# Weight splits, block-diagonal weights, rotation, modulation and skip products taken off GpSimd in a two-layer hybrid backbone

## The chip, the cores and the metric

The kernel runs on one core of one Trainium2 chip. The metric is the device time of one execution in microseconds. Before the change it is 1362.43 us, the median of three runs (1362.07 to 1367.08). The core has TensorE (matmuls into PSUM), VectorE (DVE), ScalarE (ACT), GpSimd (POOL) and SyncE (SP, which here only issues DMAs). Each has its own instruction stream, and they wait for each other by semaphores.

## The reference, cut to what matters

A diffusion backbone of two layers over 256 latent tokens behind 256 context tokens, of width 1024, all in float32:

```python
for layer in range(DEPTH):                    # DEPTH = 2
    mod = split(silu(c) @ ada_w[layer] + ada_b[layer], 6)   # for c and for c_ctx
    h = rmsnorm(x, norm_mix_w[layer]) * (1 + mod[1]) + mod[0]
    if layer % 2 == 0:   # 16 SSD heads in 4 groups beside 4 retention heads
        y = ssd_retention_mixer(h, ...)       # q, k rotated: x1 * cos - x2 * sin, ...
        #   y_ssd = scan + d_skip[:, None] * xs
    else:                # mLSTM: conv, block-wise q, k, v (512 blocks of 4 x 4), gated scan
        y = mlstm_mixer(h, ...)
    x = x + mod[2] * y
    hf = rmsnorm(x, norm_ffn_w[layer]) * (1 + mod[4]) + mod[3]
    x = x + mod[5] * ((silu(hf @ w1) * (hf @ w3)) @ w2)     # hidden width 2816
return rmsnorm(latent part of x, final_norm_w)
```

## The kernel before, in words

All 512 tokens stay in SBUF, features on the 128 partitions (`xt`, eight tiles of 128 x 512). A float32 product is made of three passes: every weight tile and every activation is split into a rounded high part and the rest (`H` and `L`), and `mm3` adds H·H, H·L and L·H in PSUM (lines 407 to 409; `mm` in the profile).

Weights come as 248 tiles of 128 x 1024 in the order of the list `plan`. `wload` issues a tile's DMA on SyncE's queue into one of three buffers `wraw`; `wprep` lets ScalarE write the high part `wH` (line 367) and VectorE or GpSimd the rest `wL` (line 368, through the helper `tt`, line 227). `wnext` keeps up to three split tiles ahead. Which engine makes `wL` is set by the tile's number:

```python
on_pool = {nz + i for i in (-15, -13, -11, -8, -6, -3, 9, 19, 25)} | {12, 14, 15, 31, 43, 56, 70, 71, 74}
...
tt(G if wpos[0] - len(wraws) - 1 in on_pool else V, L, raw, f32v(H), ALU.subtract)
```

So 18 tiles go to GpSimd. `G`, `V`, `S` and `TE` are GpSimd, VectorE, ScalarE and TensorE.

The start works through the eight feature chunks of the first normalized input in the order 3, 0, 4, 1, 5, 2, 6, 7. A chunk needs its shift and scale for both streams, four products of a weight tile with the conditioning vector. For chunks 0 to 2 TensorE makes them (`ada_rows`, line 302). For chunks 3 to 7 `ada_split` makes them, each either as one VectorE instruction that also sums over the columns (`junk<-adaf,cbc`, line 291, followed by a read of the sum) or as a GpSimd product into `ada` that ScalarE sums (line 296). The tuple `units` says how many of the four are VectorE's. Then VectorE scales the chunk (`xn`, line 487), ScalarE writes its high part (`hH`, line 497) and VectorE the rest (`hL`, line 498), and TensorE multiplies four weight tiles by it. The later modulation vectors are VectorE's in any case (`junk<-ada,cbc`, line 267).

Layer 0 then runs a list of units: projections of an SSD group or a retention head, or a quarter of the output projection. Between their matmuls `slot` advances generators that hold the scans. In `ssd_scan`, `xtok` is the group's x by tokens, `vw` its weighted copies for the states, `comb` the decay matrices times the scores, `y` (`yssd` in the profile) starts as the skip product `d_skip * x`. GpSimd also masks the decay rows (`erow`, line 750). In `ret_qk`, q and k of a head (`qkraw`) are multiplied by the cosines, a copy with swapped halves (`qksw`) by the sines.

Layer 1 has 16 feature tiles. `ml_post` runs the depthwise convolution (`conv<-xp`, line 685: four VectorE instructions per tile), splits the result (`xcH`, `xcL`) and calls `build_bd`, which spreads a tile's 4 x 4 blocks into a block-diagonal 128 x 256 matrix `bd`; `ml_head` makes the decayed attention (`earg`, normalizer `rr`) of a head, and a list written out by hand sets the order of these steps. The square sums of the norms (`acc`) and all reciprocal square roots (`rstd`, `rsr`, `rsm`, `ss`, by a power) are GpSimd's.

SyncE's order is the order of the program. On the other engines a list scheduler orders the instructions by its own estimate of their times.

Of the kernel before, what the change touches and what calls it, by code (L numbers as in the profile page):

```python
# [11 lines left out]
AF = mybir.ActivationFunctionType  # L12
ALU = mybir.AluOpType
# [4 lines left out]
P = 128  # L18
# [3 lines left out]
NCH = 4  # L22
# [140 lines left out]
RC = {"dtb": 0, "alog": 32, "ssdd": 64, "retl": 80, "gb": 88}  # L163
# [23 lines left out]
def tile_hybrid(ctx, tc, A, out, dbg=None):  # L187
    nc = tc.nc
    V, S, G, TE = nc.vector, nc.scalar, nc.gpsimd, nc.tensor
# [7 lines left out]
    def nm(p):  # L197
        uid[0] += 1
        return f"{p}_{uid[0]}"

    def const(shape, name, dt=F32, scoped=False):
        return (pool[0] if scoped else sb).tile(list(shape), dt, tag=name, name=name, bufs=1)

    def s2(p="s2", shape=(P, 512), dt=F32):
        return sb.tile(list(shape), dt, tag="s2", name=nm(p), bufs=36)

    def s4(p, shape=(P, NCH, 256)):
        return pool[0].tile(list(shape), F32, tag="s4", name=nm(p), bufs=8)

    def small(p, shape, bufs=2, dt=F32):  # L210
        return pool[0].tile(list(shape), dt, tag="sm_" + p, name=nm(p), bufs=bufs)

    def mmps(shape=(P, 512)):
        return psp.tile(list(shape), F32, tag="mm", name=nm("mm"), bufs=4)

    def scps(shape=(P, 512)):
        return psp.tile(list(shape), F32, tag="sc", name=nm("sc"), bufs=4)
# [5 lines left out]
    def f32v(t):  # L223
        return t.bitcast(F32)

    def tt(eng, o, a, b, op):
        eng.tensor_tensor(out=o, in0=a, in1=b, op=op)  # L227
# [7 lines left out]
    rowp = const([P, NROW], "rowp")  # L235
# [109 lines left out]
    plan = []  # L345
    wready = []
    wpos = [0]

    wraws = []

    def wload():
        if wpos[0] >= len(plan) or len(wraws) >= 3:
            return
        raw = sb.tile([P, 1024], F32, tag="wraw", name=nm("wraw"), bufs=3)
        nc.sync.dma_start(out=raw, in_=plan[wpos[0]])
        wpos[0] += 1
        wraws.append(raw)

    def wprep():
        if not wraws:  # L360
            wload()
        if not wraws:
            return
        raw = wraws.pop(0)
        H = sb.tile([P, 1024], F32R, tag="wH", name=nm("wH"), bufs=4)
        L = sb.tile([P, 1024], F32R, tag="wL", name=nm("wL"), bufs=4)
        S.copy(out=H, in_=raw)  # L367
        tt(G if wpos[0] - len(wraws) - 1 in on_pool else V, L, raw, f32v(H), ALU.subtract)
        wready.append((H, L))

    def wnext(ahead=3):
        while len(wready) < ahead and (wraws or wpos[0] < len(plan)):
            wprep()
        while len(wraws) < 2 and wpos[0] < len(plan):
            wload()
        return wready.pop(0)
# [5 lines left out]
    for kind, n in UNITS:  # L382
        if kind == "O":
            plan += [A["wout"][n * 4 + k] for k in range(4)]
        else:
            b = (n if kind == "G" else 4 + n) * 6
            plan += [A["win"][b + k] for k in range(2 if kind == "R" and n < 2 else 0, 6)]

    def plan_ffn(l):
        r = []  # L390
        for pi, (lo, hi) in enumerate(FPARTS):
            for m in range(lo, hi):
                r += [A["f13"][(l * KF + m) * 2], A["f13"][(l * KF + m) * 2 + 1]]
            r += [A["f2"][(l * 3 + pi) * 8 + m] for m in range(KD)]
        return r
    plan += plan_ffn(0)
    nz = len(plan) + 16
    on_pool = {nz + i for i in (-15, -13, -11, -8, -6, -3, 9, 19, 25)} | {12, 14, 15, 31, 43, 56, 70, 71, 74}
    plan += [A["wup"][m] for m in range(32)]
    plan += [A["wdn"][n] for n in range(16)]  # L400
    plan += plan_ffn(1)
# [116 lines left out]
    rope = const([P, 2, 256], "rope", scoped=True)  # L518
# [3 lines left out]
    nc.scalar.dma_start(out=cfeat, in_=A["cfeat"].rearrange("p (a b) -> p a b", a=KD))  # L522
    S.activation(cfeat, cfeat, AF.Silu)
    seq = (3, 0, 4, 1, 5, 2, 6, 7)
    units = (4, 2, 3, 2, 3,)
    at, ar = {}, {}

    def ld(i):
# [32 lines left out]
    tt(V, accs.acc, accs.acc, accs.parts(ALL)[1], ALU.add)  # L561
    ra = rstd_a([accs.acc], 0, 4, 1.0 / D, RMS_EPS, True)
    wprep()
    prep(0)
    rb = rstd_b(ra, 4)
# [196 lines left out]
    def ssd_proj(g):  # L762
        fs = []
        for t in (8 + g, 12 + g, 2 * g, 2 * g + 1):
            _, o = conv(projA(hs), "cw", "cb", t)
            S.activation(o, o, AF.Silu)
            fs.append(o.rearrange("p a b -> p (a b)"))
            slot()
        zs = s4("zs")

        def ev(c, p):
            S.activation(zs[:, c, :], p, AF.Silu)
        projB(hs, ev)
        bg.add(ssd_scan(g, fs, zs), True)

    def ssd_scan(g, fs, zs):
# [4 lines left out]
        xtok = s4("xtok")  # L781
        for half in range(2):
            p = scps([P, 2, 256])
# [24 lines left out]
        for c in range(NCH):  # L808
            m = comb[(g, c)]
            tt(V, m, m, sT[:, c, :].unsqueeze(1).to_broadcast([P, 4, P]), ALU.mult)  # L810
        y = s4("yssd")
        tt(G, y.rearrange("p c (h e) -> p c h e", h=4), xtok.rearrange("p c (h e) -> p c h e", h=4),
           rowp[:, RC["ssdd"] + 4 * g:RC["ssdd"] + 4 * g + 4].unsqueeze(1).unsqueeze(3).to_broadcast([P, NCH, 4, 64]),
           ALU.mult)
        yield
        st = []
        for n in range(3):
            p = scps([P, 2, 256])
# [51 lines left out]
    def ret_qk(ps):  # L870

        qk = []
        raw = s2("qkraw", (P, 2, 256))
        for n, sc in ((0, 1.0), (1, 128 ** -0.5)):
            p = ps[n]()
            t = s2("qT")
            S.activation(t[:, CT_], p[:, CT_], AF.Copy, scale=sc)
            S.activation(raw[:, n, :], p[:, LT_], AF.Copy, scale=sc)
            qk.append(t)
        sw = s2("qksw", (P, 2, 256))  # L880
        nc.sync.dma_start(out=sw[0:64], in_=raw[64:128])
        nc.sync.dma_start(out=sw[64:128], in_=raw[0:64])
        tt(G, raw, raw, rope[:, 0, :].unsqueeze(1).to_broadcast([P, 2, 256]), ALU.mult)
        tt(V, sw, sw, rope[:, 1, :].unsqueeze(1).to_broadcast([P, 2, 256]), ALU.mult)
        for n in range(2):
            tt(V, qk[n][:, LT_], raw[:, n, :], sw[:, n, :], ALU.add)
        return qk

    def ret_proj(h, pre=None):
        ready = {}  # L890
        bg.add(ret_scan(h, ready), True)

        def pa():
            p = projA(hs)
            slot()
            return p
        qk = ret_qk((pa, pa)) if pre is None else pre
        vt = s4("vt")
        gs = s4("gs")
        projB(hs, lambda c, p: S.activation(gs[:, c, :], p, AF.Silu))  # L900
        ready["qk"] = qk
        projB(hs, lambda c, p: S.copy(out=vt[:, c, :], in_=p))
        ready["vg"] = (vt, gs)
# [136 lines left out]
    def out_quarter(q):  # L1040
        while any(q * 4 + k not in yT for k in range(4)):
            bg.step()
        for mp in range(4 if q < 3 else 2):
            w = wnext()
            for m2 in range(2):
# [6 lines left out]
                slot()  # L1052

    pre = [ret_qk((lambda: p4[2 * h], lambda: p4[2 * h + 1])) for h in range(2)]
    bg.add(dt_chain())
    for kind, n in UNITS:
# [28 lines left out]
    def build_bd(t):  # L1085

        o = small("bd", [P, 2 * P + 16], 2)
        tt(G, o[:, 0:2 * P].rearrange("p (a b c) -> p a b c", a=2, c=4),
           bdc[:, t].unsqueeze(2).to_broadcast([P, 2, 32, 4]), bm4, ALU.mult)
        V.tensor_copy(out=o[:, 2 * P:], in_=gvw[:, t])  # L1090
        return o
# [374 lines left out]
    for pi, (lo, hi) in enumerate(FPARTS):  # L1466
# [11 lines left out]
        for m in range(KD):  # L1478
            if ps2:
                p = ps2.pop(0)  # L1480
            else:
                w = wnext()
                p = mmps([P, 256])
# [6 lines left out]
    for m in range(KD):  # L1490
        o = s2("fin")[:, :256]
# [22 lines left out]
```

## Time and profile before

| | |
|---|---|
| median of the runs | 1362.43 us |
| profiled execution | 1364.7 us, span of its instructions 1362.9 us, mean granted TensorE clock 0.986 |
| TensorE | 1315.0 us, 96% of the span |
| VectorE | 960.6 us, 70%, 1653 instructions |
| ScalarE | 643.1 us, 47%, 1110 instructions |
| GpSimd | 221.5 us, 16%, 186 instructions |
| HBM read | 197.16 MB, 145 GB/s over the span |

[...] In rows of groups, line, engine, operation, output and inputs, shape and count are followed by the busy time in us, the mean of one in ns, and the idle time of the engine before them with what ended it. In rows of the order of time, the first number is the start from the span's begin, the second the duration, in us; x2 joins two neighbours. In rows of waits stand the waiting instruction, what it waited for, the total in us, how many times, and the longest. Matmuls overlap, so a matmul of 512 columns reads as 0.39 us though one starts every 0.23 us.

### The profile page before, as it was taken

What the parts mean: (1) busy time and instruction counts of PE and PEld (TensorE: products, weight loads), DVE (VectorE), ACT (ScalarE), POOL (GpSimd) and SP (SyncE); (2) the same over time, 40 slices, a digit from 0 to 9 for tenths busy, and PEclk for the clock granted to TensorE, in tenths of its full rate; (3) what the DMA queues carried; (4) which work ended last, traced back from release to release, by engine and by line L of the source; (5) the groups of instructions that cost most, each with busy time, mean ns of one, the idle gap of its engine ahead of it and who ended that gap; (6) DMA issues with size and microseconds to landing.
All of it is one profiled execution on the core that took longest, in us unless ns stands there. A gap on an engine that the chain in (4) does not pass through costs nothing.

```text
span 1362.9 us, 21033 instructions
## 1 busy us (share of the span) xinstructions
PE 1315.0 (96%) x8158; PEld 1150.2 (84%) x8158; DVE 960.6 (70%) x1653; ACT 643.1 (47%) x1110; POOL 221.5 (16%) x186
## 2 busy tenths in 40 slices
PE   6999999999999999999999999989999999999997
PEld 2599878887899888888888888889999678999997
DVE  7988797875867568898556633586666996565655
ACT  4466747655754344221222133455565664444443
POOL 2234141512122031000000120512110011000001
PEclk9999999999999999999999999999999999899998
DMA  9246453534412224556547622411114424365553
GB/s 364 93 155 188 128 197 101 170 109 139 155 62 72 89 96 158 197 203 245 186 170 247 238 98 104 140 63 47 63 63 139 141 91 148 120 202 201 193 198 118
DMA packets 60837, 200.70 MB, mean 147 GB/s; under 512 B 6841, under 2 KB 8377, under 8 KB 60737
## 3 DMA queue, kind: packets, MB, share of 16 engines
q1 hardware_dynamic: 60594, 199.36, 42.7%
q8 instruction: 64, 1.05, 0.3%
q14 instruction: 35, 0.29, 0.1%
q10 hardware_dynamic: 144, 0.01, 0.0%
HBM read 197.16 MB, written 1.13 MB: 145 GB/s over the span
## 4 chain that ended last, share of the span: by engine, by line
PE 77%; DVE 9%; issue 6%; ACT 3%; DMA 2%; POOL 1%; POOLq 0%; SPq 0%; DVEq 0%; ACTq 0%
PE mm L407 23%; PE mm L408 23%; PE mm L409 23%; DVE wL L227 1%; DMA erow<-scr 1%; PE mm L1217 1%; PE sc L1345 1%; PE sc L838 1%; PE sc L956 1%; DVE junk L267 1%; DVE conv L685 1%; ACT wH L367 1%; PE sc L820 1%; POOL wL L227 1%; DVE earg L1316 1%
## 5 line engine op out<-in xcount | busy, mean ns | idle before, releaser
L367 ACT CAST wH<-wraw 128x1024 fp32r<-128x1024 f32 x248 | 259.1, 1048 | 410.5 <-PE mm L408 278.6
L227 DVE TENSOR_TENSOR wL<-wraw,wH 128x1024 fp32r<-128x1024 f32 x230 | 288.4, 1256 | 130.0 <-ACT wH L367 122.9
L409 PE MATMUL mm<-hH,wL 128*128 128x512 f32 (+1 forms) x568 | 219.9, 388 | 1.3 <-DVE wL L227 1.3
L408 PE MATMUL mm<-hL,wH 128*128 128x512 f32 (+1 forms) x568 | 220.2, 388 | 0.4 <-DVE hL L498 0.4
L407 PE MATMUL mm<-hH,wH 128*128 128x512 f32 (+1 forms) x568 | 218.4, 389 | 0.0
L267 DVE SCALAR_TENSOR_TENSOR junk<-ada,cbc 128x1024 bf16<-128x1024 f32 x128 | 164.6, 1286 | 17.4 <-DMA ada<-in_ada 16.1
L409 PEld LDWEIGHTS mm<-hH,wL 128*128 128x128 f32 x568 | 107.9, 190 | 25.5 <-DVE wL L227 1.8
L408 PEld LDWEIGHTS mm<-hL,wH 128*128 128x128 f32 x568 | 107.8, 190 | 24.1 <-DVE hL L498 0.6
L407 PEld LDWEIGHTS mm<-hH,wH 128*128 128x128 f32 x568 | 106.7, 189 | 23.3
L685 DVE SCALAR_TENSOR_TENSOR conv<-xp,prm,conv 128x512 f32<-128x512 f32 x128 | 107.4, 843 | 21.2 <-ACT conv L682 20.2
L981 DVE SCALAR_TENSOR_TENSOR xt<-mm,mod,xt 128x256 f32<-128x256 f32 x144 | 64.6, 479 | 66.3 <-PE mm L409 66.2
L407 PE MATMUL mm<-wH,hH 128*128 128x256 f32 x384 | 110.8, 289 | 0.0
L408 PE MATMUL mm<-hp,wH 128*128 128x256 f32 x384 | 107.8, 282 | 1.1 <-DVE hp L498 1.1
L407 PE MATMUL mm<-hp,wH 128*128 128x256 f32 x384 | 108.1, 286 | 0.0
L408 PE MATMUL mm<-wL,hH 128*128 128x256 f32 x384 | 108.0, 282 | 0.0
L409 PE MATMUL mm<-wH,hL 128*128 128x256 f32 x384 | 107.8, 281 | 0.0
L409 PE MATMUL mm<-hp,wL 128*128 128x256 f32 x384 | 107.6, 282 | 0.0
L407 PE MATMUL mm<-hHL,wH 128*128 128x256 f32 x352 | 97.8, 280 | 1.1 <-ACT hHL L497 1.1
L408 PE MATMUL mm<-hHL,wH 128*128 128x256 f32 x352 | 98.1, 279 | 0.0
L409 PE MATMUL mm<-hHL,wL 128*128 128x256 f32 x352 | 98.0, 279 | 0.0
L407 PEld LDWEIGHTS mm<-hp,wH 128*128 128x128 f32 x384 | 72.9, 192 | 3.2 <-ACT conv L682 2.0
L408 PEld LDWEIGHTS mm<-hp,wH 128*128 128x128 f32 x384 | 73.6, 192 | 1.9 <-DVE hp L498 1.3
(333 smaller groups left out, 2987.9 us busy)
## 6 DMA issues: line engine op xcount, KB each, us to landing
wraw<-in_f SPq DMA_DIRECT2D x136, 512.0 KB, 3.7
ada<-in_ada SPq DMA_DIRECT2D x80, 512.0 KB, 4.5
wraw<-in_win SPq DMA_DIRECT2D x48, 512.0 KB, 4.7
wraw<-in_wup SPq DMA_DIRECT2D x32, 512.0 KB, 3.3
erow<-scr SPq DMA_DIRECT2D x16, 512.0 KB, 6.9
wraw<-in_wout SPq DMA_DIRECT2D x16, 512.0 KB, 3.9
wraw<-in_wdn SPq DMA_DIRECT2D x16, 512.0 KB, 3.9
adaf<-in_ada SPq DMA_DIRECT2D x10, 512.0 KB, 6.8
```

The source lines that it names most:

```text
L227: eng.tensor_tensor(out=o, in0=a, in1=b, op=op)
L267: V.scalar_tensor_tensor(out=junk, in0=raw, scalar=1.0, in1=cbc[:, st, :], op0=ALU.mult, op1=ALU.mult, accum_out=mod[l][c][:, k, st:st + 1])
L367: S.copy(out=H, in_=raw)
L407: TE.matmul(o, lhsT=lh, rhs=rh, start=first and i == 0, stop=False)
L408: TE.matmul(o, lhsT=lh, rhs=rl, start=False, stop=False)
L409: TE.matmul(o, lhsT=ll, rhs=rh, start=False, stop=last and i == n - 1)
L685: V.scalar_tensor_tensor(out=o, in0=x[:, :, k:k + 256], scalar=pc(wname, t * 5 + k), in1=o, op0=ALU.mult, op1=ALU.add)
L820: TE.matmul(p[:, d, :], lhsT=btok[:, c, :], rhs=vws[n][:, d, :], start=True, stop=True)
L838: TE.matmul(p1[:, i, h * 64:(h + 1) * 64], lhsT=comb[(g, c0 + i)][:, h, :], rhs=xtok[:, c0 + i, h * 64:(h + 1) * 64], start=True, stop=True)
L956: TE.matmul(py[:, i, :], lhsT=src[:, i * P:(i + 1) * P], rhs=vt[:, j, :], start=j == 0, stop=j == len(srcs) - 1)
L981: V.scalar_tensor_tensor(out=xt[:, m, half], in0=p[:, o:o + 256], scalar=gate[:, m, st:st + 1], in1=xt[:, m, half], op0=ALU.mult, op1=ALU.add)
L1217: TE.matmul(pv[:, c, :], lhsT=xm[:, c0 // 2, 2 + c * P:2 + (c + 1) * P], rhs=b[:, P:], start=True, stop=True)
```

## The change

GpSimd gives up five kinds of work. The splits of 18 weight tiles, the block-diagonal products of all 16 tiles of layer 1, the cosine products of the four heads and six modulation products of the start go to VectorE; the last also take a column sum each from ScalarE, since VectorE's form makes the sum itself. The skip product of each of the four SSD groups becomes four ScalarE instructions, one per head, with the head's factor as a scale. Line numbers after it are two lower from line 397 on.

```diff
-        tt(G if wpos[0] - len(wraws) - 1 in on_pool else V, L, raw, f32v(H), ALU.subtract)
+        tt(V, L, raw, f32v(H), ALU.subtract)
...
-    nz = len(plan) + 16
-    on_pool = {nz + i for i in (-15, -13, -11, -8, -6, -3, 9, 19, 25)} | {12, 14, 15, 31, 43, 56, 70, 71, 74}
...
-    units = (4, 2, 3, 2, 3,)
+    units = (4, 4, 4, 4, 4)
...
         y = s4("yssd")
-        tt(G, y.rearrange("p c (h e) -> p c h e", h=4), xtok.rearrange("p c (h e) -> p c h e", h=4),
-           rowp[:, RC["ssdd"] + 4 * g:RC["ssdd"] + 4 * g + 4].unsqueeze(1).unsqueeze(3).to_broadcast([P, NCH, 4, 64]),
-           ALU.mult)
+        for h in range(4):
+            S.activation(y[:, :, h * 64:(h + 1) * 64], xtok[:, :, h * 64:(h + 1) * 64], AF.Copy,
+                         scale=rowp[:, RC["ssdd"] + 4 * g + h:RC["ssdd"] + 4 * g + h + 1])
...
-        tt(G, raw, raw, rope[:, 0, :].unsqueeze(1).to_broadcast([P, 2, 256]), ALU.mult)
+        tt(V, raw, raw, rope[:, 0, :].unsqueeze(1).to_broadcast([P, 2, 256]), ALU.mult)
...
-        tt(G, o[:, 0:2 * P].rearrange("p (a b c) -> p a b c", a=2, c=4),
+        tt(V, o[:, 0:2 * P].rearrange("p (a b c) -> p a b c", a=2, c=4),
            bdc[:, t].unsqueeze(2).to_broadcast([P, 2, 32, 4]), bm4, ALU.mult)
```

The scheduler makes new orders of it. SyncE's order keeps its rows. VectorE in the start, from the second modulation chunk on (`mod_81` and `mod_82` are the first layer's shift and scale, `hL_197` is the second chunk's rest, `hL_205` the third's), before:

```order
L227 TENSOR_TENSOR mod_81<-mod_81,prm 128x2
L328 SCALAR_TENSOR_TENSOR amix_93<-mod_82,prm 128x2
L487 SCALAR_TENSOR_TENSOR xn_258<-xt,amix_93,sc_185 128x256 x2
L227 TENSOR_TENSOR mod_82<-mod_82,prm 128x2
L498 SCALAR_TENSOR_TENSOR hL_197<-xn_258,mod_81,hH_196 128x256
L328 SCALAR_TENSOR_TENSOR amix_93<-mod_82,prm 128x2
L498 SCALAR_TENSOR_TENSOR hL_197<-xn_258,mod_81,hH_196 128x256
L487 SCALAR_TENSOR_TENSOR xn_294<-xt,amix_93,sc_185 128x256 x2
L227 TENSOR_TENSOR wL_313<-wraw_221,wH_312 128x1024
L498 SCALAR_TENSOR_TENSOR hL_205<-xn_294,mod_81,hH_204 128x256 x2
```

and after:

```order
L291 SCALAR_TENSOR_TENSOR junk_245,mod_81<-adaf_126,cbc 128x1024
L328 SCALAR_TENSOR_TENSOR amix_93<-mod_82,prm 128x2
L291 SCALAR_TENSOR_TENSOR junk_247,mod_82<-adaf_128,cbc 128x1024
L485 SCALAR_TENSOR_TENSOR xn_256<-xt,amix_93,sc_185 128x256 x2
L227 TENSOR_TENSOR mod_81<-mod_81,prm 128x2
L227 TENSOR_TENSOR mod_82<-mod_82,prm 128x2
L496 SCALAR_TENSOR_TENSOR hL_197<-xn_256,mod_81,hH_196 128x256
L328 SCALAR_TENSOR_TENSOR amix_93<-mod_82,prm 128x2
L227 TENSOR_TENSOR wL_311<-wraw_221,wH_310 128x1024
L496 SCALAR_TENSOR_TENSOR hL_197<-xn_256,mod_81,hH_196 128x256
L485 SCALAR_TENSOR_TENSOR xn_292<-xt,amix_93,sc_185 128x256 x2
L291 SCALAR_TENSOR_TENSOR junk_318,mod_81<-adaf_262,cbc 128x1024
```

Two modulation products now stand ahead of the second chunk's `xn`, the third weight split stands between the halves of its `hL`, and a further product ahead of the third chunk's `hL`.

VectorE at the first feature tiles of layer 1 (`conv_7934`, after the change `conv_7940`, is the first tile's convolution), before:

```order
L227 TENSOR_TENSOR wL_7955<-wraw_7774,wH_7954 128x1024
L685 SCALAR_TENSOR_TENSOR conv_7934<-xp_555,prm,conv_7934 128x512 x4
L227 TENSOR_TENSOR wL_8192<-wraw_7958,wH_8191 128x1024
L227 TENSOR_TENSOR gm<-mm_8030,rowp 128x32
L1090 COPY bd_8063<-blk_4882 128x16
L227 TENSOR_TENSOR xcL_7942<-conv_7934,xcH_7941 128x512
```

and after:

```order
L227 TENSOR_TENSOR wL_7961<-wraw_7780,wH_7960 128x1024
L683 SCALAR_TENSOR_TENSOR conv_7940<-xp_549,prm,conv_7940 128x512 x2
L227 TENSOR_TENSOR wL_8077<-wraw_7782,wH_8076 128x1024
L683 SCALAR_TENSOR_TENSOR conv_7940<-xp_549,prm,conv_7940 128x512
L227 TENSOR_TENSOR gm<-mm_8036,rowp 128x32
L683 SCALAR_TENSOR_TENSOR conv_7940<-xp_549,prm,conv_7940 128x512
L227 TENSOR_TENSOR gm<-mm_8041,rowp 128x32
L227 TENSOR_TENSOR bd_8069<-blk_4888,cst 128x256
L1088 COPY bd_8069<-blk_4888 128x16
L227 TENSOR_TENSOR wL_8198<-wraw_7964,wH_8197 128x1024
L227 TENSOR_TENSOR xcL_7948<-conv_7940,xcH_7947 128x512
```

A split that GpSimd made beside the convolution (`wL_8077`) stands in its midst, and the third tile's block-diagonal product ahead of `xcL`.

VectorE at the first head's attention of layer 1 (`negm` is the running maximum, `den` the normalizer's sum, a row with `negm` alone reads an accumulator), before:

```order
L1316 ISA earg_9716,negm_9714<-urow_9710,mmask_7924 128x512
L1316 ISA negm_9714 128x1
L1316 ISA earg_9720,negm_9714<-urow_9711,mmask_7925 128x512
L1316 ISA negm_9714 128x1
L1316 ISA earg_9734,negm_9732<-urow_9710,mmask_7926 128x512
L1316 ISA negm_9732 128x1
L1319 SCALAR_TENSOR_TENSOR earg_9716,den_9715<-earg_9716,S_8475 128x512
```

and after:

```order
L1314 ISA earg_9722,negm_9720<-urow_9716,mmask_7930 128x512
L1314 ISA negm_9720 128x1
L227 TENSOR_TENSOR wL_9803<-wraw_9688,wH_9802 128x1024
L1317 SCALAR_TENSOR_TENSOR earg_9722,den_9721<-earg_9722,S_8481 128x512
L1314 ISA earg_9726,negm_9720<-urow_9717,mmask_7931 128x512
L1314 ISA negm_9720 128x1
L1314 ISA earg_9740,negm_9738<-urow_9716,mmask_7932 128x512
```

The split `wL_9803` that GpSimd made before stands behind the first row of the head.

## The prediction

> **What bounds the kernel now.** I read the busy shares first, then TensorE's waits, then the stretches, and last the order of time around the longest waits.
>
> ```profile
> PE 1315.0 (96%) x8158; PEld 1150.2 (84%) x8158; DVE 960.6 (70%) x1653; ACT 643.1 (47%) x1110; POOL 221.5 (16%) x186
> PEclk9999999999999999999999999999999999899998
> ...
> 25.00:65.00 40.00, 34.94 (x134) 20.35 (x133) 39.00 (x81) 15.69 (x32) 13.52 (x5) 0.91 0.46 174
> 1080.00:1110.00 30.00, 28.71 (x159) 20.53 (x158) 28.80 (x76) 17.85 (x37) 4.48 (x3) 1.00 0.44 140
> ```
>
> TensorE is busy 96% of the span, so work on another engine counts only where TensorE waits for it. VectorE, 70% over the whole, is full in two stretches (39.00 of 40 us, 28.80 of 30; columns: PE, PEld, DVE, ACT, POOL, clock, DMA). TensorE's waits say who is late:
>
> ```profile
> PE sc L820 <- DVE vw L227: 5.3, 3, 2.6
> PE sc L1227 <- ACT xcH L1198: 3.9, 1, 3.9
> PE sc L587 <- DVE hL L498: 3.8, 3, 2.9
> PE sc L439 <- POOL rstd L227: 3.5, 3, 1.4
> PE sc L1336 <- DVE rr L227: 3.5, 2, 3.2
> ...
> PE mm L409 <- DVE wL L227: 1.3, 1, 1.3
> ...
> PE mm L408 <- DVE hp L498: 1.1, 1, 1.1
> ```
>
> Most name VectorE (xcH is ScalarE's copy of what VectorE's conv leaves). These six rows without rstd make 18.9 us: the change can win in them and in what they hold up.
>
> **What GpSimd does to VectorE.** The order of time at the start shows it.
>
> ```profile
> 21.20 5.12 POOL L227 TENSOR_TENSOR ada<-adaf,cbc 128x1024 f32<-128x1024 f32 x2 [4.46 <-DMA adaf<-in_ada]
> 34.88 5.92 POOL L227 TENSOR_TENSOR ada<-adaf,cbc 128x1024 f32<-128x1024 f32 x2 [2.87 <-ACT arow L305]
> ...
> 21.09 2.99 DVE L498 SCALAR_TENSOR_TENSOR hL<-xn,mod,hH 128x256 fp32r<-128x256 f32 x2 [0.18 <-ACT hH L497]
> 24.00 3.40 DVE L227 TENSOR_TENSOR wL<-wraw,wH 128x1024 fp32r<-128x1024 f32 x1
> 29.80 2.22 DVE L227 TENSOR_TENSOR mod<-mod,prm 128x2 f32<-128x2 f32 x1
> 35.97 5.11 DVE L498 SCALAR_TENSOR_TENSOR hL<-xn,mod,hH 128x256 fp32r<-128x256 f32 x2
> 51.67 2.41 DVE L227 TENSOR_TENSOR mod<-mod,prm 128x2 f32<-128x2 f32 x2
> 58.17 0.88 DVE L498 SCALAR_TENSOR_TENSOR hL<-xn,mod,hH 128x256 fp32r<-128x256 f32 x2
> 63.57 0.48 DVE L498 SCALAR_TENSOR_TENSOR hL<-xn,mod,hH 128x256 fp32r<-128x256 f32 x1
> ```
>
> A pair of hL takes 0.88 us at 58.17 with GpSimd idle, and 5.11 at 35.97 with GpSimd in two products, ending as they end (40.8 against 41.1). A product on two columns takes 2.22. VectorE does not share, it stands, and so does every engine behind it. [...] By its opposite, a shared port at half speed, the five rows could hold only 0.9 + 1.3 + 0.2 + 0.9 + 0.2 = 3.5 us of waits against 7.8 of new work, and the sum below would fall from 12.8 to 4.3 us. The trace agrees with the first: 5.11 is six times 0.88.
>
> **The change part by part.** Removed from GpSimd, and the prices of what comes instead:
>
> ```profile
> L227 POOL TENSOR_TENSOR wL<-wraw,wH 128x1024 fp32r<-128x1024 f32 x18 | 46.2, 2570 | 130.5 <-ACT wH L367 130.5
> L227 POOL TENSOR_TENSOR ada<-adaf,cbc 128x1024 f32<-128x1024 f32 x6 | 17.3, 2898 | 19.9 <-ACT ada L296 10.3 <-DMA adaf<-in_ada 6.8 <-ACT arow L305 2.9
> L227 POOL TENSOR_TENSOR bd<-blk,cst 128x256 f32<-128x256 f32 x16 | 16.3, 1020 | 72.2 <-PE mm L1217 62.1 <-ACT wH L367 7.1 <-DVE blk L1116 3.0
> L227 POOL TENSOR_TENSOR yssd<-xtok,rowp 128x1024 f32<-128x1024 f32 x4 | 8.7, 2180 | 37.5 <-issue 21.2 <-ACT xtok L787 16.3
> L227 POOL TENSOR_TENSOR qkraw<-qkraw,rope 128x512 f32<-128x512 f32 x4 | 6.0, 1512 | 33.3 <-ACT wH L367 17.3 <-DMA qksw<-qkraw 11.2 <-ACT gs L900 4.7
> ...
> L227 DVE TENSOR_TENSOR wL<-wraw,wH 128x1024 fp32r<-128x1024 f32 x230 | 288.4, 1256 | 130.0 <-ACT wH L367 122.9 <-PE mm L1217 2.5 <-PE sc L942 0.8
> L291 DVE SCALAR_TENSOR_TENSOR junk<-adaf,cbc 128x1024 bf16<-128x1024 f32 x14 | 17.1, 1219 | 0.1
> L227 DVE TENSOR_TENSOR yo<-yo,xt 128x256 f32<-128x256 f32 x8 | 3.4, 421 | 0.0
> L227 DVE TENSOR_TENSOR acc<-acc,sq 128x512 f32<-128x512 f32 x7 | 4.8, 692 | 7.5 <-ACT sq L453 7.4
> L864 ACT ACTIVATE yssd<-yssd,ss 128x256 f32<-128x256 f32 x16 | 6.8, 498 | 4.4 <-POOL ss L227 4.3
> ```
>
> GpSimd gives up 46.2 + 17.3 + 16.3 + 8.7 + 6.0 = 94.5 us. VectorE takes on 18 splits at 1.256 (22.6), six modulation products at about 1.30 with the read of the sum (7.8), 16 bd at 0.42 (6.7; yo is the nearest shape) and four rotations at 0.69 (2.8; acc): 39.9 us. ScalarE takes on 16 products at 0.50 (8.0) and drops six sums over 1024 columns. TensorE's instructions and the DMAs are the same in kind and number. Against VectorE's 39.9 us stand at most 94.5 us of standing still. What counts is where.
>
> *Start (the six ada products).* Waits that vanish: hL 2.99 - 0.88 = 2.1; wL 3.40 - 1.26 = 2.1; mod 2.1; hL 5.11 - 0.88 = 4.2; mod 2.2: 12.7 us. Added 7.8. VectorE's stream, unbroken up to the last hL (63.57 + 0.48 = 64.05), would be 4.9 us shorter. The new order puts the third split between the two halves of the second hL, and two products ahead of its xn; walking it with the durations above I get the last hL at 59.9. I take 4.2 us; bounds 0 (TensorE has no slack to use it) and 7.
>
> *The other five places.* Each row of VectorE below stands or comes late behind a GpSimd instruction that the change removes.
>
> ```profile
> 171.14 2.91 DVE L227 TENSOR_TENSOR wL<-wraw,wH 128x1024 fp32r<-128x1024 f32 x1
> 246.11 5.05 DVE L227 TENSOR_TENSOR comb<-comb,sT 128x512 f32<-128x512 f32 x4
> 254.76 1.50 DVE L227 TENSOR_TENSOR vw<-xtok,wdec 128x256 f32<-128x256 f32 x1
> 878.15 2.74 DVE L498 SCALAR_TENSOR_TENSOR hp<-xn,mod,hp 128x256 fp32r<-128x256 f32 x2
> 896.80 5.39 DVE L685 SCALAR_TENSOR_TENSOR conv<-xp,prm,conv 128x512 f32<-128x512 f32 x4
> 1049.79 2.24 DVE L1316 CUSTOM_DVE_ANT_0 earg<-urow,mmask 128x512 f32<-128x512 f32 x1 [1.33 <-DMA urow<-scr]
> 1101.01 2.31 DVE L227 TENSOR_TENSOR rr<-rr,den 128x2 f32<-128x2 f32 x1
> ...
> 179.37 0.89 PE L820 MATMUL sc<-vw,btok 128*128 128x256 f32 x3 [2.34 <-DVE vw L227]
> ...
> 869.97 1.77 POOL L227 TENSOR_TENSOR rstd<-rstd,mhalf 128x2 f32<-128x2 f32 x1 [3.29 <-DVE rstd L431]
> ```
>
> 171: 2.91 - 1.26 = 1.7 us less and no split added; TensorE waits 2.34 us for the vw behind it: I take 1.7, bounds 0 and 2.3. 246 to 256: comb loses 5.05 - 4 x 0.69 = 2.3 and vw 1.50 - 0.42 = 1.1, 3.4 in all, cut to the 2.6 that TensorE's longest wait for vw shows; bounds 0 and 2.6. 878: hp loses 2.74 - 0.88 = 1.9, but a split of 1.26 now stands ahead of it: 0.6, bounds 0 and 1.1. 896: conv loses 5.39 - 4 x 0.69 = 2.6 and gets a split in its midst: 1.3, bounds 0 and 3.9. 1049 and 1101, the attention of the second layer: earg loses 2.24 - 0.69 = 1.5, rr about 2.1 (it writes two columns); each gets a split: 0.3 + 0.9. In the new order TensorE has 16 projection matmuls ahead of the first transposes that wait there, which fill part of the 3.2 us for rr; I add 1.2. Together 2.4, bounds -1 and 5. The other splits, bd and the four rotations lie where TensorE has other work and waits for nothing; I cost them at nothing, and if that cover goes, their price is 1.26 us a split.
>
> ScalarE's skip products (four of 0.50 us per group) stand ahead of a copy of the scores or of the states; the products themselves are read only after matmuls that follow these. Nothing, bounds 0 and 2 us (one group of four in TensorE's way).
>
> Sum: 4.2 + 1.7 + 2.6 + 0.6 + 1.3 + 2.4 = 12.8 us. The profiled execution took 1364.7 us (span 1362.9 and 1.8 around it), so 1351.9; it lies 2.3 us over the median 1362.43, so 1349.6 against the median. With the lower and upper ends the gain lies between -1 - 2 = -3 and 7 + 2.3 + 2.6 + 1.1 + 3.9 + 5 = 21.9 us.
>
> **The rivals.** *The clock comes back too.* In 25:65 TensorE was granted 0.91 of its clock: 3.6 us of 40. Where its waits go, that loss may go. The upper ends with it make 25.5 us: 1337. For it: the dips in the clock row's stretch and at the end lie beside waits. Against: the second dip in 25:65 comes where TensorE is already fed. [...]
>
> *The waits only change their owner.* VectorE stays full in 25:65 and 1050:1110, now with its own products, and selects and sums that remain on GpSimd still stop it. If the start gives 2 us and the other places half of their terms, the gain is 2 + 4.3 = 6.3; if only the start gives, 2 to 4. I put it at 4 us: 1358.4. For it: 28.80 of 30 us. Against: at each place but 1049 the wait removed is longer than the work put in. [...]
>
> *Slower: VectorE stops GpSimd.* The lock works both ways: the rstd at 869.97 takes 1.77 us where a split runs on VectorE. GpSimd keeps every power (rstd, rsr, rsm, ss), on which TensorE waits at the ends of stages. Each of the 18 new splits can hold one such step for 1.26 us, 22.7 in all: 1372. It needs 11 of 18 caught on TensorE's path to eat the 12.8, and 16 to be seen as slower. Against: TensorE waits for rstd three times only, 3.5 us. [...]
>
> **How the numbers follow.** Forecast (gain 6.8 to 19) 0.58; the clock too 0.13; owner changed 0.23; slower 0.06. The time is that of the first, 1349.6, its own range 1343.5 to 1355.6. For 8 in 10, half of the second and half of the third come in: 1337 to 1359. A difference of 0.5% (6.8 us) is about what these runs can tell from none. Faster by more: 0.58 + 0.13 + 0.05 of the third = 0.76; the rest of the third, 0.18, is the same; slower 0.06.
>
> **What would show it.** GpSimd's busy time falls from 221.5 to about 127 us. VectorE's busy time stays near 950, since what it no longer stands is about what it takes on; the mean of its splits falls from 1256 to near 1220 ns, and pairs of hL take 0.9 us all through the start. The last hL of the start comes near 60 us, not 64. TensorE's rows for vw, hL and wL shrink to under 2 us each, that of xcH to 2.6; rr stays above 1. Wrong, if the last hL stays at 64 or TensorE runs out of work elsewhere before 65 us; if the row of TensorE on rstd grows past 5 us; or if new rows name VectorE's wL in 500:870, where I count 1.26 us a split as hidden.

## The result, and the profile after

The changed kernel takes 1347.74 us (median of four runs, 1344.61 to 1349.42); the kernel before, now with four runs, 1364.76. The ratio is 0.9857, with a 95% interval of 0.9825 to 0.9889: 19.5 us faster, at least 15 (the two medians themselves are 17.0 us apart). The forecast was 1349.6, a gain of 12.8. The profiled execution has a span of 1342.8 us, 20.1 less than before; it is the fastest of the four. One execution of a kernel below (the skip product alone, 1862.11 us) ran at a granted clock of 0.655 throughout and is left out of all comparisons.

The busy times and the clock row of the changed kernel's page:

```profile
PE 1308.1 (97%) x8158; PEld 1147.5 (85%) x8158; DVE 945.6 (70%) x1703; ACT 643.2 (48%) x1114; POOL 124.8 (9%) x138
PEclk9999999999999999999999999999999999899998
```

GpSimd lost 96.7 us. VectorE has 50 instructions more and is busy 15 us less, because it stands less, and an instruction that stands counts as busy (the pair of hL at 35.97 before, with 5.11 us). What TensorE waits for now (instruction, cause, total us, times, longest; the rows on which the prediction bears):

```profile
PE mm L405 <- ACT xcH L1196: 4.4, 1, 4.4
PE sc L437 <- POOL rstd L227: 3.8, 4, 1.4
...
PE sc L1334 <- DVE earg L1327: 2.8, 2, 2.5
...
PE sc L584 <- ACT hH L495: 1.9, 1, 1.9
PE sc L732 <- ACT yssd L862: 1.9, 1, 1.9
PE sc L423 <- POOL acc L227: 1.6, 2, 1.0
...
PE mm L406 <- DVE hL L496: 0.4, 1, 0.4
```

The rows for vw (5.3), wL (1.3) and hp (1.1) are gone and that for hL fell from 3.8 to 0.4. Those for hH at the start (0.7 before) and for yssd (1.2 before) grew. xcH did not shrink (3.9 before). The row for rr became one for earg, the instruction next to it in the same chain.

Stretches of before and of after show which places gained (columns: PE, PEld, DVE, ACT, POOL, clock, DMA). First before, then after:

```profile
165.00:185.00 20.00, 17.31 (x92) 14.21 (x91) 19.90 (x35) 9.19 (x17) 8.01 (x4) 1.00 0.53 184
240.00:262.00 22.00, 19.36 (x110) 17.14 (x109) 19.08 (x26) 13.78 (x27) 9.99 (x9) 0.92 0.61 188
870.00:910.00 40.00, 33.27 (x252) 32.22 (x251) 32.57 (x57) 21.96 (x42) 13.85 (x9) 0.91 0.35 119
```

```profile
25.00:65.00 40.00, 36.58 (x160) 24.41 (x159) 36.22 (x96) 15.38 (x33) 0.00 (x0) 0.96 0.46 177
165.00:185.00 20.00, 20.00 (x96) 16.45 (x96) 20.00 (x38) 11.62 (x26) 3.26 (x4) 1.00 0.60 168
240.00:262.00 22.00, 22.00 (x163) 21.04 (x162) 21.08 (x43) 16.27 (x34) 6.25 (x5) 1.00 0.61 180
870.00:910.00 40.00, 35.21 (x269) 32.69 (x268) 31.65 (x65) 24.95 (x50) 0.71 (x1) 0.96 0.20 67
```

In the first two stretches after the start TensorE now works without a break. VectorE is as full as before or fuller (21.08 of 22 us against 19.08): the time that it stood is filled with the work that it took on.

Where the 20 us came from is found by laying the two traces on a scale of TensorE's work: each matmul counts the median distance from one of its shape to the next, and the gain at a place is by how much earlier the changed kernel reaches the same amount of work. In us of before; "forecast" is the prediction's term:

| place | 0-20 | 20-140 | 140-240 | 240-400 | 400-860 | 860-880 | 880-1040 | 1040-1160 | 1160-1180 | sum |
|---|---|---|---|---|---|---|---|---|---|---|
| gained | 0.6 | 5.7 | 3.1 | 3.5 | 0.5 | 1.9 | 1.7 | 1.4 | 1.6 | 19.9 |
| forecast | | 4.2 | 1.7 | 2.6 | 0 | 0.6 | 1.3 | 2.4 | 0 | 12.8 |

### The profile page after: what moved, and what is told of

Read it like the earlier page. It is cut to its first block, busy times and chain, and to the rows that moved or that the text cites. A ratio compares the mean times of both kernels' runs of the same rounds, so it can differ in the third digit from the quotient of the medians.

```text
span 1342.8 us, 20999 instructions
## 1 busy us (share of the span) xinstructions
PE 1308.1 (97%) x8158; PEld 1147.5 (85%) x8158; DVE 945.6 (70%) x1703; ACT 643.2 (48%) x1114; POOL 124.8 (9%) x138
## 4 chain that ended last, share of the span: by engine, by line
PE 82%; DVE 7%; issue 4%; DMA 2%; ACT 2%; POOL 1%; SPq 0%; POOLq 0%; DVEq 0%; ACTq 0%
PE mm L405 24%; PE mm L406 24%; PE mm L407 24%; DVE wL L227 2%; PE sc L954 2%; PE mm L1215 1%; ACT wH L367 1%; PE sc L836 1%; DVE junk L291 1%; DMA ada<-in_ada 1%; DMA wraw<-in_wup 1%; PE sc L841 1%; PE sc L818 1%; DVE junk L267 1%; PE sc L732 1%
## 5 line engine op out<-in xcount | busy, mean ns | idle before, releaser
L227 DVE TENSOR_TENSOR wL<-wraw,wH 128x1024 fp32r<-128x1024 f32 x248 | 305.1, 1232 | 139.6 <-ACT wH L367 129.7
L267 DVE SCALAR_TENSOR_TENSOR junk<-ada,cbc 128x1024 bf16<-128x1024 f32 x128 | 157.9, 1233 | 19.6 <-DMA ada<-in_ada 18.1
L683 DVE SCALAR_TENSOR_TENSOR conv<-xp,prm,conv 128x512 f32<-128x512 f32 x128 | 96.5, 757 | 14.8 <-ACT conv L680 13.8
L405 PEld LDWEIGHTS mm<-hp,wH 128*128 128x128 f32 x384 | 72.6, 191 | 2.7 <-ACT conv L680 1.1
L405 PE MATMUL mm<-uH,wH 128*128 128x512 f32 (+1 forms) x200 | 73.6, 368 | 0.0
```

What stands on the lines that cost most here:

```text
L267: V.scalar_tensor_tensor(out=junk, in0=raw, scalar=1.0, in1=cbc[:, st, :], op0=ALU.mult, op1=ALU.mult, accum_out=mod[l][c][:, k, st:st + 1])
L405: TE.matmul(o, lhsT=lh, rhs=rh, start=first and i == 0, stop=False)
L683: V.scalar_tensor_tensor(out=o, in0=x[:, :, k:k + 256], scalar=pc(wname, t * 5 + k), in1=o, op0=ALU.mult, op1=ALU.add)
```

## The experiments

What the expectations call the port theory is the prediction's reading of its rows: a VectorE instruction stands still while GpSimd runs (5.11 us for a pair of hL that takes 0.88 with GpSimd idle), and what the change gains is what VectorE no longer stands ahead of TensorE's waits. What the two engines share is seen in no run; port is only a name for it. The rivals: GpSimd's results were merely late; ScalarE was relieved; or the new order as a whole did it. In the expectations, "before" is the kernel before, and gains are counted against it.

### Each part alone

The start alone (`units = (4, 4, 4, 4, 4)` in the kernel before):

> The kernel before, with only the six modulation products of the start moved to VectorE. Port theory (VectorE stands while GpSimd runs a product; the places are independent): the start gains what it gained under the whole change, 5.5 to 6.5 us on TensorE's path by 70 us, the other places nothing, total 1356 to 1357 against 1362.4. Order theory (the whole order counts, VectorE was full in 25:65 and stays full): 0 to 2 us.

The splits alone (`tt(V, L, raw, f32v(H), ALU.subtract)` for all tiles):

> The kernel before, with only the 18 weight splits moved to VectorE. Port theory: gains where a split of GpSimd held VectorE ahead of TensorE: near 878 about 1.9 us, near 896 1.3, at 1049 and 1101 together 1.5 to 3, and a part of the 4 us at 246 to 256; 5 to 8 us in all, and nothing at 171 or in the start. Rival (VectorE's 22.6 us of new splits come onto the path once GpSimd has gone): 0 or a loss.

The skip product alone (four ScalarE products in place of GpSimd's one):

> The kernel before, with only the skip product moved to ScalarE. Port theory: the split at 171 no longer stands for 1.7 us, TensorE's wait of 2.34 us for vw behind it goes: 1.7 to 3 us there, 1 to 2 us at 246, together 3 to 5 us. Rival (ScalarE's four products of 0.50 us per group delay the copies behind them): 0 to -2 us.

Block-diagonal and rotation products alone (`tt(V, ...)` in `build_bd` and `ret_qk`):

> The kernel before, with only the block-diagonal and the rotation products moved to VectorE. Port theory: vw at 254.76 loses the 1.1 us that it stood behind a rotation, worth 1 to 3 us with the clock step behind it; the block-diagonal products, 0 to 0.5 us, since TensorE waits there for little. Together 1 to 3 us. With e1 to e3 the four gains should add up to about 19 us if the places are independent; if the order of the whole decides, they do not.

Measured against the kernel before, five rounds each: start 0.9963 (0.9941 to 0.9986), splits 0.9930 (0.9907 to 0.9954), skip 0.9959 (0.9937 to 0.9980), block-diagonal and rotation 1.0006 (0.9988 to 1.0024). In us of 1366: 5.0, 9.6, 5.6 and -0.8. The product of the four ratios is 0.9859; the whole change has 0.9857. The totals add up, within their intervals. The start is a little under the 5.5 to 6.5 us expected; the splits are the largest part and, like the skip product, a little more than expected; the block-diagonal and rotation products are worth nothing, below the 1 to 3 us expected.

By place, worked out as in the table above (the skip product from its second profile, below):

| place | whole change | start | splits | skip | bd, rotation |
|---|---|---|---|---|---|
| 20-140 | 5.7 | 5.0 | 0.2 | 0.5 | 0.0 |
| 140-240 | 3.1 | -2.2 | -1.3 | 1.9 | 0.2 |
| 240-400 | 3.5 | 0.7 | 3.2 | 2.8 | 0.7 |
| 860-880 | 1.9 | 0.0 | 1.9 | 0.0 | 0.0 |
| 880-1040 | 1.7 | -1.7 | -0.5 | 0.2 | -1.7 |
| 1040-1160 | 1.4 | 0.3 | 1.7 | -1.2 | -1.5 |
| 1160-1180 | 1.6 | 0.0 | 1.3 | 1.5 | 1.5 |

Each of the three parts that gain does so where its GpSimd instruction stood: the start in the start, the skip product at 171, the splits at 878. The 1.3 us that the splits were expected to gain near 896 did not come (880 to 1040 loses 0.5). At 246 the splits and the skip product each win about 3 us, and both together 3.5: there the same wait can be won once. So place by place the parts do not add up, and that their totals come so close is in part chance. The losses of 1.2 to 2.2 lie where nothing was changed, but for the 1.7 of the block-diagonal products in their own stretch; in each of these stretches that profile has one or two half-clock steps of TensorE that the profile of before does not have (last section). For example the start alone at its wait for vw, which is no longer than before (4.8 us in all, 5.3 before): here the stretch behind it runs at half clock, before it did not. The start alone, then the kernel before at the same place:

```profile
175.51:178.92 3.41, 2.90 (x8) 2.35 (x8) 3.41 (x7) 3.41 (x10) 1.49 (x2) 0.50 0.18 75
```

```profile
178.06:181.47 3.41, 1.75 (x7) 1.31 (x8) 3.41 (x10) 3.35 (x9) 1.08 (x2) 1.00 0.58 225
```

The skip product alone was profiled a second time:

> The kernel before with the skip product on ScalarE, profiled once more, since the first profile was taken at two thirds of the clock throughout. Port theory: TensorE's wait for vw at 176 goes (2.3 to 3 us), 1 to 2 us at 246, and the start and layer 1 stay as before.

One run, 1358.23 us. VectorE's split no longer stands (order of time; 2.91 us at 171.14 before), and TensorE's row for vw is 2.1 us in all against 5.3:

```profile
170.34 1.22 DVE L227 TENSOR_TENSOR wL<-wraw,wH 128x1024 fp32r<-128x1024 f32 x1
```

```profile
PE sc L820 <- DVE vw L227: 2.1, 2, 1.6
```

The gain at 140 to 240 is 1.9 (2.3 to 3 expected), at 246 it is 2.8 (1 to 2 expected).

### Is it VectorE's standing, or GpSimd's slowness?

In the changed kernel GpSimd again makes the 18 differences, but nobody reads them:

```diff
         tt(V, L, raw, f32v(H), ALU.subtract)
+        if wpos[0] - len(wraws) - 1 in on_pool:
+            tt(G, sb.tile([P, 960], mybir.dt.bfloat16, tag="idle", ...), raw[:, 0:960], f32v(H)[:, 0:960], ALU.subtract)
```

> The changed kernel, in which GpSimd also makes the 18 differences it used to make (960 of 1024 columns, rounded to bfloat16) into a tile that nobody reads; VectorE still makes its own. The orders of TensorE, VectorE and ScalarE are those of the changed kernel, row by row. Port theory: VectorE stands beside them, its busy time rises by 15 to 25 us, and 4 to 9 us of the 9.5 us that the splits alone gave are lost again: 1352 to 1357 us. Rival (what counted was GpSimd's own slow result or the new order): nothing waits for these, 1346 to 1349.5.

And the same with a copy, `G.tensor_copy(out=..., in_=raw[:, 0:960])`:

> The same with a copy of 960 columns (one SBUF input) in place of the difference (two). If two inputs make VectorE stand: VectorE's busy time rises by at most 8 us and the time by 0 to 2.5 us. If any GpSimd instruction at these places does: as with the differences, 15 to 25 us of VectorE and 4 to 9 us of time.

The differences: 1371.67 us, ratio 1.0026 (1.0006 to 1.0046). Against the changed kernel's 0.9857 that is 1.7%, some 23 us: the gain of the whole change is lost, although nobody reads the 18 results and the other engines run the same instructions in the same order. Late results of the splits and the order are excluded as causes of this loss. The differences are not quite alone, though: GpSimd's own later work stands behind them (its square sums acc start at 874.18, as the difference of 870.91 ends, and TensorE's row for acc is 3.5 us against 1.6), and a buffer that GpSimd still reads is refilled later (SyncE waits 16.7 us in 8 waits for that, but no row of TensorE names a weight's DMA). The page, and the order of time at two of the places:

```profile
PE 1323.1 (96%) x8158; PEld 1158.8 (84%) x8158; DVE 972.9 (71%) x1703; ACT 643.0 (47%) x1114; POOL 178.5 (13%) x156
L227 POOL TENSOR_TENSOR idle<-wraw,wH 128x960 bf16<-128x960 f32 x18 | 52.5, 2915 | 217.5 <-ACT wH L367 187.6
```

```profile
107.61 2.31 POOL L227 TENSOR_TENSOR idle<-wraw,wH 128x960 bf16<-128x960 f32 x1 [7.87 <-ACT wH L367]
107.82 3.18 DVE L267 SCALAR_TENSOR_TENSOR junk<-ada,cbc 128x1024 bf16<-128x1024 f32 x1
...
899.64 3.23 POOL L227 TENSOR_TENSOR idle<-wraw,wH 128x960 bf16<-128x960 f32 x1 [13.77 <-issue]
900.71 2.70 DVE L688 SCALAR_TENSOR_TENSOR conv<-xp,prm,conv 128x512 f32<-128x512 f32 x1
```

```profile
PE mm L410 <- ACT xcH L1201: 6.4, 1, 6.4
...
PE sc L823 <- DVE vw L227: 4.2, 3, 3.0
PE sc L1339 <- DVE earg L1332: 3.6, 2, 3.4
...
PE sc L428 <- POOL acc L227: 3.5, 2, 2.5
```

VectorE's product of 1.22 us takes 3.18, a convolution step of 0.75 takes 2.70, and GpSimd's own difference 3.23 in place of 2.31 where VectorE was first. VectorE's busy time rises by 27.3 us, a little over the 15 to 25 expected. The loss of time was expected at 4 to 9 us and came out at 23. By place this profile (span 1376.3 us) loses some 27 us ahead of 1180 against the changed kernel, most of it at 140 to 240 (some 7) and at 880 to 1040 (some 9), and some 6 more in a slower last stretch (last section). Two things make it more than expected. A stretch in which VectorE stands is not over when GpSimd is done: at 170 no difference is anywhere near (GpSimd is idle from 150 to 177), and still TensorE waits 3.0 us for vw again. VectorE is 7.6 us behind the changed kernel right after the differences of 128 (a convolution step at 137.10 against 129.47) and still 7.6 us behind at vw (176.65 against 169.04). And there are twelve half-clock steps of TensorE where the changed kernel has seven (mean granted clock 0.983 against 0.988); at 1.7 us each at most (last section) they are up to 8.5 of the 27 us.

Which instructions of VectorE stand can be read inside one difference:

```profile
527.19 2.64 POOL L227 TENSOR_TENSOR idle<-wraw,wH 128x960 bf16<-128x960 f32 x1 [1.17 <-ACT wH L367]
527.63 0.67 DVE L227 TENSOR_TENSOR u<-u,mm 128x512 f32<-128x512 f32 x1
528.23 2.69 DVE L227 TENSOR_TENSOR wL<-wraw,wH 128x1024 fp32r<-128x1024 f32 x1
```

The product u<-u,mm has one of its inputs in PSUM and takes its usual time inside the difference. The split behind it has both in SBUF and loses 1.47 us (2.69 against 1.22) of the 1.60 that the difference still has to go. In the kernel before it is the same: 30 VectorE instructions with an input in PSUM began inside a GpSimd product, sum or difference that had at least 0.3 us to go, and none took over 0.02 us more than usual. Of those with two inputs in SBUF, the 49 that have a usual time to compare with took 0.18 to 2.19 us more. Six copies with one input in SBUF took 0.25 to 0.42 us more, so a second input is not needed for it. Beside GpSimd's powers (rstd, rsr, ss) none of VectorE's stood: eight instructions with two inputs in SBUF took at most 0.01 us more, such as the product at 15.87, 1.22 us with 0.86 of a power to go.

The copies: 1353.87 us, ratio 0.9891 (0.9859 to 0.9922), 4.6 us over the changed kernel's, which the two intervals do not tell apart for sure. VectorE's busy time is 951.7, 6.1 more. So VectorE's time lies where the expectation put it if the copy's one input spares VectorE, and the 4.6 us lie where it put them if it does not: the times do not decide. The trace does. A copy stops VectorE like a difference does, only for a shorter time:

```profile
88.69 1.00 POOL L370 CAST idle<-wraw 128x960 bf16<-128x960 f32 x1 [2.86 <-DMA wraw<-in_win]
...
88.77 2.00 DVE L267 SCALAR_TENSOR_TENSOR junk<-ada,cbc 128x1024 bf16<-128x1024 f32 x1
```

1.22 plus 0.78, where the copy had 0.92 to go. The price grows with the length of the GpSimd instruction, but not in proportion to it: the 18 differences are 52.5 us of GpSimd and added 27.3 us to VectorE's busy time, the copies 21.8 and 6.1.

### Was ScalarE relieved?

In the kernel before, the six products of the start are made by VectorE, and ScalarE still sums them (`tt(V, pr, raw, cbc[:, st, :], ALU.mult)` in `ada_split`):

> The kernel before, in which VectorE makes the six modulation products of the start as plain products and ScalarE still makes their six sums. Port theory: most of the gain of the start alone (5.0 us), less what the longer chain costs, 3 to 5 us: 1358 to 1360 beside 1363. Rival (ScalarE was freed of six sums): nothing, or a loss, 1362 to 1365.

Ratio 0.9953 (0.9929 to 0.9978), 6.4 us faster, more than the 3 to 5 expected, where the start alone has 0.9963; the intervals overlap. The whole gain is there with ScalarE's six sums still in place. By place it is 5.8 us in 20 to 140. No gain of ScalarE's relief can be seen.

### What did VectorE's new splits cost?

```diff
-        L = sb.tile([P, 1024], F32R, tag="wL", ...)
         S.copy(out=H, in_=raw)
-        tt(V, L, raw, f32v(H), ALU.subtract)
+        L = H
+        if wpos[0] - len(wraws) - 1 not in on_pool:
+            L = sb.tile([P, 1024], F32R, tag="wL", ...)
+            tt(V, L, raw, f32v(H), ALU.subtract)
```

> The changed kernel without the 18 splits that VectorE took over: those tiles have no low part, and their third pass multiplies by the high part instead (the same matmuls, so the results differ). TensorE's order is the same but for some ten rows. The prediction priced these 22.6 us of VectorE at about 2 us on TensorE's path; by that, 1 to 4 us faster than the changed kernel, 1342 to 1347. Rival (half of the added work is on the path, and the splits gained 9.5 us only as a balance): 8 to 12 us faster, 1335 to 1340.

1346.47 us, ratio 0.9853 (0.9822 to 0.9884), beside 0.9857: VectorE is busy 19.6 us less (926.0), and nothing to be told from the noise is gained. As a whole the new splits are hidden, as costed. By place it is less simple. At the first feature tiles they do cost: TensorE's wait for xcH is 1.6 us without them and 4.4 with them. But this kernel's own order loses as much at 270, where VectorE stands behind GpSimd's sums yssd + yst; this kernel's waits:

```profile
PE sc L736 <- ACT yssd L866: 4.7, 1, 4.7
PE sc L1229 <- ACT xcH L1200: 1.6, 1, 1.6
```

### A further step

The changed kernel with the twelve sums yssd + yst on VectorE too (`tt(V, yv, yv, t, ALU.add)`):

> The changed kernel with the twelve sums of the SSD outputs (yssd + yst) on VectorE as well. They held VectorE for 2.55 us in all, and TensorE waits 2.0 us at 269.7 behind the chain that they are in. Port theory: 1 to 3 us faster than the changed kernel, most of it near 270. Rival (VectorE is full there, 21.1 of 22 us in 240 to 262): no change, or up to 2 us slower.

1344.89 us, ratio 0.9828 (0.9798 to 0.9858), 4 us under the changed kernel's ratio; the intervals overlap, and the two profiled spans are the same (1342.9 and 1342.8), so a gain in time is not shown. At the place itself there is one: the changed kernel, then this one, at the same split:

```profile
262.09 2.99 POOL L227 TENSOR_TENSOR yssd<-yssd,yst 128x512 f32<-128x512 f32 x2 [0.18 <-DVE yst L227]
263.86 2.30 DVE L227 TENSOR_TENSOR wL<-wraw,wH 128x1024 fp32r<-128x1024 f32 x1
```

```profile
266.79 0.68 DVE L227 TENSOR_TENSOR yssd<-yssd,yst 128x512 f32<-128x512 f32 x1
267.40 1.22 DVE L227 TENSOR_TENSOR wL<-wraw,wH 128x1024 fp32r<-128x1024 f32 x1
```

TensorE's wait for yssd falls from 1.9 to 1.2 us, and the half-clock step at 273 is gone; by place 240 to 400 gains 6.4 us against before, where the changed kernel gains 3.5. In this profile as much is lost in small pieces elsewhere. VectorE was 21.1 of 22 us full there and still had room: in 240:276 it is busy 32.96 us with the sums and 33.00 without, so here they took no longer than it had stood for them. Over the whole kernel it is not so; the twelve sums take 9.5 us of VectorE, and its busy time rises by 3.8. Whether VectorE's standing or GpSimd's longer sum on the way to yssd (1.74 us at 260.18, against 0.68) made the wait, this run does not tell.

To this the block-diagonal products were put back on GpSimd:

> The changed kernel with the twelve SSD sums on VectorE, and the block-diagonal products back on GpSimd. Port theory: each holds VectorE for 0.35 us and saves it 0.42, so within 1.5 us of the kernel with the sums alone (0.9828 of before). Rival (VectorE has room in layer 1 and the port does not count there): the same; only a difference above 3 us would tell against both.

1346.30 us, ratio 0.9858 (0.9823 to 0.9893). The ratio is 4 us over that of the kernel with the sums alone, where 1.5 were expected, but the medians are 1.4 us apart and the intervals overlap: it cannot be told from that kernel, nor from the changed one, and nothing speaks for it. Since it has the twelve sums too, it does not support a gain in time from them either; at the place itself it has it again (6.3 us in 240 to 400).

## Why the prediction was right, and which terms were off

*The mechanism* is right and shown: differences on GpSimd that nobody reads bring the loss back, and each part that gains does so where its GpSimd instruction stood. Half speed, the prediction's opposite, is out: the split at 528.23 above lost 1.47 us of the 1.60 that the difference had to go, where half speed would have cost half of it, 0.80. *The time* came out 1.9 us from the forecast, the gain 6.7 us. The forecast counted from 1362.43 us; from the median of four runs it would have been 1351.9, so part of the nearness in time is luck. *The signs* came as named, with three exceptions: GpSimd 124.8 us (127 forecast), VectorE 945.6 (950), hL in pairs of 0.87 to 0.88 throughout the start, rstd at 3.8 (under 5), no row on wL in 500:870. The exceptions: xcH is 4.4 us and not 2.6; rr's row became one for earg; and TensorE did run out of work at a new place before 65 us (1.9 us for hH at 49.2), which the prediction had named as a sign of being wrong. The last hL of the start is over at 57.7 (60 forecast; 64.05 before), and the mean split takes 1232 ns, not 1220, since GpSimd's remaining sums and masks still hold some of them (2.30 us for the split at 263.86 beside a sum, 1.64 for the one at 110.16 beside a mask). The last hL:

```profile
57.23 0.48 DVE L496 SCALAR_TENSOR_TENSOR hL<-xn,mod,hH 128x256 fp32r<-128x256 f32 x1
```

*The sum* was 12.8 against some 19.5, and the terms failed in these ways:

- *Start*, 4.2 forecast, 5.7 measured. VectorE got 2.2 us further than the walk through its new order said. For a time the gain was larger still (8.5 us at 56 us of before), and 3 us went back where ScalarE's hH became the late one (1.9 us at 49.2) and a half-clock step followed.
- *171*, 1.7 forecast, 3.1 measured. The lower of two figures was taken (what VectorE stood); TensorE's whole wait of 2.3 us went, and the 0.4 us behind it.
- *246 to 256*, 2.6 forecast, 3.5 measured: 4.4 by 260, of which 1 went back by 320 (the wait for yssd at 270 and the half-clock step behind it). Here the clock rival was right: the step at 256.6 vanished, and 0.92 became 1.00.
- *878*, 0.6 forecast, 1.9 measured, all of it from the splits alone. The step that failed: only VectorE's wait for GpSimd was priced. GpSimd's own queue was not. Its square sums acc stood behind its splits (873.01 and 877.85 before), and TensorE waits for acc; that row fell from 2.6 to 1.6 us, in the splits alone too:

```profile
PE sc L425 <- POOL acc L227: 1.6, 2, 1.0
```

- *896*, 1.3 forecast, and the wait for xcH, to shrink to 2.6 us, is 4.4. The chain from the first convolution step to xcH did get shorter, from 6.84 us (896.80 to 903.64) to 5.78 (882.33 to 888.11). But it starts 14.5 us earlier than before where TensorE is there 16.1 us earlier, and TensorE waits the more. The forecast priced the chain and forgot that its beginning does not move with TensorE's gains. The 1.7 us of this stretch are clock: the step at 881.2 has no counterpart.
- *1049 and 1101*, 2.4 forecast, 1.4 measured: 2.1 gained at 1101, and 0.7 lost at 1049, where earg now waits behind a split on its own engine and a half-clock step follows.
- *1160 to 1180*, nothing forecast, 1.6 measured, and it is no work of the change: the waits are the same two before and after, but the profile of before has three half-clock steps there and the changed kernel's two. Of thirteen profiles of this case, nine have two and four have three: this term is luck.

Of the rivals, the clock is the one that came in part: nine half-clock steps (those at the very end left out) became seven. A step of 3.41 us at half clock costs at most half of itself, 1.7 us, so the two are some 3 of the 20 us, an estimate. The prediction held against it that the second dip in 25:65 comes where TensorE is fed again; but that step, at 41.52, begins right behind the 2.9 us wait for hL, which ends at 41.1. The chance of 0.13 was low for steps that can go one at a time. The owners of the waits did change (hH, yssd, earg), which the third rival named, but took back some 5 us and not half of the gain. VectorE's lock on GpSimd came to nothing: 3.5 us of waits for rstd became 3.8.

## What to carry to other kernels

In these runs a difference, product or sum of GpSimd beside VectorE instructions that read SBUF alone was paid twice: by its own length, and by VectorE's standing for up to that length (27.3 us for 52.5 us of differences). By this, handing such work to an idle GpSimd pays only where VectorE has nothing from SBUF alone to do, or where nobody is behind it. Look for it in the order of time as VectorE instructions of a multiple of their usual length that end with a GpSimd instruction. And price a removed instruction in both queues that it held, VectorE's and its own engine's.

## What the runs showed of the hardware

*Half-clock steps lie on a grid.* In the profiles of before and of after all stretches at a granted clock of 0.50 begin at a multiple of 3.41 us from each other, and ahead of the very end they last one to three such steps. From before, then from after:

```profile
27.87:31.28 3.41, 3.41 (x10) 1.01 (x10) 3.41 (x7) 0.00 (x0) 2.63 (x1) 0.50 1.03 417
41.52:44.93 3.41, 3.41 (x10) 2.35 (x8) 3.41 (x10) 0.00 (x0) 0.00 (x0) 0.50 0.09 36
1164.51:1174.75 10.24, 8.09 (x37) 7.61 (x38) 6.24 (x17) 3.32 (x8) 0.70 (x1) 0.50 0.19 63
```

```profile
887.82:891.23 3.41, 3.07 (x12) 2.52 (x13) 2.98 (x7) 2.64 (x6) 0.00 (x0) 0.50 0.43 155
1044.84:1048.25 3.41, 3.41 (x19) 3.41 (x18) 3.41 (x11) 3.41 (x7) 0.00 (x0) 0.50 0.37 145
1147.24:1154.07 6.83, 4.68 (x21) 4.20 (x21) 4.54 (x13) 2.54 (x6) 0.70 (x1) 0.50 0.25 82
```

41.52 is 4 steps after 27.87, 1164.51 is 333 steps. In the changed kernel a step in which TensorE was out of work for 1.9 us (from 48.15, busy 1.47 of 3.41) or 2.5 (from 1041.43, busy 0.90) was followed by one at half clock, while 3.2 us from 1057.1 before, split by the grid into 1.6 and 1.6, cost nothing more. No single length parts the two: 1.7 us inside the step at 178.06 before (its row stands above, TensorE busy 1.75 of 3.41) was followed by a full one, 1.3 us inside the step at 488.47 after (busy 2.13) by one at half clock. So a wait cost its length alone, or by the estimate above up to 1.7 us more for each half-clock step behind it, and where it lay on the grid decided in part. The changed kernel profiled again:

> The changed kernel, profiled a second time. If the half-clock steps of 3.41 us lie on a grid of their own that does not start with the kernel, the waits are the same as in the first profile and the steps stand at other places, so that the span moves by some 1.7 us a step; if they belong to the waits, they stand behind the same waits.

1347.96 us, span 1346.2, with nearly the same waits but for yssd (3.5 us) and earg (its longest 1.7 us, 2.5 in the first profile). The grid lies 1.0 us later against the kernel's start: the first three steps begin at 52.57, 274.43 and 492.89, where the first profile has them at 51.56, 273.43 and 491.88. Behind them it has steps at 868 and 892 and none at 1044:

```profile
868.35:871.76 3.41, 3.41 (x18) 3.41 (x17) 3.41 (x10) 1.82 (x4) 0.00 (x0) 0.50 0.94 330
1044.84:1048.25 3.41, 2.05 (x18) 1.84 (x16) 3.28 (x11) 2.80 (x8) 0.00 (x0) 1.00 0.22 89
```

So most steps stand behind waits, but not behind each wait, they begin on a grid that does not start with the kernel, and which wait gets one changes from run to run.

*A slower last stretch.* In four profiles (the splits alone, both of the idle GpSimd instructions, and the one without the 18 splits) TensorE starts 4% fewer matmuls from about 1180 us on, at a granted clock of 1.00; the changed kernel, then the one with idle differences:

```profile
1200.00:1300.00 100.00, 100.00 (x885) 100.00 (x884) 60.56 (x74) 45.39 (x59) 0.00 (x0) 1.00 0.57 194
```

```profile
1200.00:1300.00 100.00, 100.00 (x852) 100.00 (x851) 57.75 (x73) 44.66 (x62) 0.00 (x0) 1.00 0.58 188
```

It is worth some 6 us of these spans. It comes and goes with the execution: the kernel without the 18 splits took 1353.8 us in its profiled one and 1346.1 to 1346.6 in its five others. Its cause is open. The places above are compared ahead of it.
